# Gates' stage of a hybrid decoder block: the order of its products and weight sums, mixed results loaded as whole tiles, low parts on VectorE

## The chip, the cores and the metric

The kernel runs on one core of one Trainium2 chip. The time is that of one execution on the device, in microseconds (us), the median of several runs. The profile comes from one profiled execution of the kernel before the change, and every time below is from that execution unless it is called a median.

The names of the profile: PE is TensorE's matmul, PEld its weight load, DVE is VectorE, ACT is ScalarE, POOL is GpSimd, SP is SyncE, which issues nearly all DMAs. L255 is line 255 of the kernel.

## The reference

One decoder block on x of 2048 tokens by 1024 channels, all in float32. Cut to what matters:

```python
h = rmsnorm(x, attn_norm)
z = h @ w_in                         # pool | q | k | v | gate_pool | gate_attn
g_pool, g_attn = split(sigmoid(z[gates] + b_gate))
a = pool_mixer(u_pool, w_pool, pool_scale)
b = swa_sink_attention(rope(rmsnorm(q)), rope(rmsnorm(k)), v, sinks)   # window 128
x = x + (g_pool * a + g_attn * b) @ w_out
h = rmsnorm(x, ffn_norm)
up = causal_depthwise_conv(h @ w_up, conv_w, conv_b)
x = x + (silu(up[gate half]) * up[value half]) @ w_down
```

There are 16 query heads and 2 key and value heads of 64 channels, d_ff is 2816, and the pooling windows are 2, 4, 8 and 16.

## The kernel before

**Number format.** A float32 operand is split in a high part (a cast to float32r on ScalarE) and a low part (the operand less its high part, a subtraction on VectorE). A product is made of three matmuls: high by high, high by low, low by high. `split` (L229 to L234) makes both parts of a weight tile in two halves: L232 is the cast, L233 the subtraction. `split_added` (L236 to L240) makes the low part in another way, for the tiles of `pu` (eight), `q` (the first four), `ga` and `pg` (two each): ScalarE writes the high part (L238) and the negative of the high part (L239 copies with scale -1), and GpSimd issues a DMA (L240) that reads the weights again from memory and adds them. Only chunk 0 makes these tiles; chunk 1 loads the made ones back.

**Tiling and stages.** The tokens are cut in two chunks of 1024. Each chunk goes through: keys, values and queries, sliding-window attention with projections between its steps (`project` at L255, scores at L868, exponentials at L887, the probabilities' transposes at L901 and their copies at L903 and L906, GpSimd's select of the window's edge at L909, the values at L929); the Gates' stage; the output projection (`out_proj`, also L255); the up-projection; and the down-projection. Up and gates use a seven-product scheme for a 2 by 2 block product: each pair of output slabs needs the products "one" to "seven" (`class Up`), each of 12 matmuls of 512 columns, issued at L1164 in `product`.

**The Gates' stage.** It works through six units, u0 to u5, in the order of `UNITS`. A unit makes the two gates (attention and pool) of one slab of 128 channels. Its products add on PSUM banks: "one", "three", "five" and "seven" on one bank (`self.x`), each but the last two copied off by ScalarE (L1182, `kept`) before the next one writes; "four" and "six" on another (`self.z`), "four" copied off; "two" on a third. `early` is "six" issued ahead of its sum. VectorE adds the partial sums (L1194, L1208, L1220), and `sigmoid` multiplies by the norm's factor (L1370), takes tanh on ScalarE (L1371) and multiplies into the attention or pool result (L1372). `combine` (L1381) adds both and stores the slab to `xd` in memory. `fetch` loads the pool result `dd` and the attention result `tad`.

**Operands of that stage.** The left operands are sums of weight blocks, made by `Blocks` in four steps (L356 is the cast, L357 the subtraction for its low part, L372 and L373 the same for `A22`, L376 to L385 the sums). `weights(f, n)` runs n more steps for unit f. The right operands are blocks of the input, loaded by `load_input` (1 MB each), scaled by `scale_input` (L1406), combined (`right_t2`, `right_t3`, `right_t4`) and split by `parted` (L1039 the cast, L1040 the low part).

**The output projection.** It makes two halves of 512 tokens (n = 0, 1) by eight slabs (m). Each needs the four mixed results of that half in parts. Those of the first half are made at the end of the Gates' stage, those of the second at m = 1 to 4 of the first half: `mixed(j, n)` loads 512 KB of `xd` into an M tile and splits it.

**What sets the order.** Every engine runs its instructions in program order. A scheduler at build time interleaves the streams from the order of the code and the tile pools: "U" with 19 tiles of 1 MB, "M" with 5, "F" with 4, "R" with 3, "Q" with 6, and two PSUM banks each for f, a and t. A pool hands its slots out in the order of allocation, and a new tile waits for the last use of the slot's old one, be that a DMA.

Of the kernel before, what the change touches and what calls it, by code (L numbers as in the profile page):

```python
# [26 lines left out]
P = 128  # L27
D = 1024
S = 2048
T = 1024  # L30
# [175 lines left out]
def block_kernel(ctx: ExitStack, tc: tile.TileContext, x, xT, pos, vec, qkn, w_poolT, w_pool, w_q, w_kv,  # L206
# [21 lines left out]
    def split(hi, lo, src):  # L228
        n = src.shape[1] // 2  # L229
        for i in range(2):  # L230
            t = slice(i * n, (i + 1) * n)
            high = A.copy(hi[:, t], src[:, t])  # L232
            low = V.tensor_sub(lo[:, t], src[:, t], hi[:, t].bitcast(F32))  # L233
        return high.ins, low.ins  # L234

    def split_added(hi, lo, src, again):  # L236

        A.copy(hi, src)  # L238
        A.activation(lo, src, AF.Copy, scale=-1.0)  # L239
        G.dma_start(lo, again.bitcast(F32R), accum_op=ALU.add)  # L240

    def halves(h, t, src, gain):

        A.activation(h[:, 0, t], src, AF.Identity, scale=gain)
# [46 lines left out]

    def split_weights(key, raws):
        if key[0] in ("up", "gates"):
            return Blocks(raws)
        if key[0] == "none":
            return None
        out = []
        if raws is None:
            for src in made[key]:
                out.append(up_.tile(list(src.shape), F32R, "U"))  # L300
                load(out[-1].bitcast(F32), src)
            return out if len(out) > 1 else out[0]
        for raw in raws:
            shape = [P, 2] + list(raw.shape)[1:]
            p, tag = (mp, "M") if out and key[1] not in FOLDS[:FOLD_LEAD] else (up_, "U")
            out.append(p.tile(shape, F32R, tag))
# [29 lines left out]
    class Blocks:  # L336
# [23 lines left out]
        def step(self, n=1):  # L360
            for _ in range(n):
                if self.at < 4:
                    (self.first, self.second, self.third, self.fourth)[self.at]()
                    self.at += 1

        def first(self):
# [65 lines left out]
    class Input:  # L432
# [8 lines left out]
        def pair(self, j, n):  # L441
            return self.t[j, n]

        def fresh(self, k, n):
            if k % 2 == 0:
                self.t[k // 2, n] = up_.tile([P, 2, 2, 512], F32R, "U")
            return self.at(k, n)

    def make_h(c, n, hs, ks=range(KT)):

        a, b = ((0, 256), (256, 512), (512, T))[n] if c == 0 else (0, T)
        for k in ks:
            gain = vc[:, V_AN + k:V_AN + k + 1]
            if c == 0:
                h = hs.at(k, 0) if n == 1 else hs.fresh(k, n // 2)
                halves(h, slice(a % 512, a % 512 + b - a), xs0[k // 2][:, k % 2, a:b], gain)
            else:
                src = mp.tile([P, T], F32, "M")
                load(src, xT[k * P:(k + 1) * P, c * T:(c + 1) * T])
                for i in range(2):  # L460
                    halves(hs.fresh(k, i), slice(0, 512), src[:, 512 * i:512 * i + 512], gain)

    both = up_.tile([P, 2, 4, 2 * P], F32, "U")

# [586 lines left out]
    def out_proj(c, ms):  # L1051

        xg = [up_.tile([P, 2, T], F32, "U") for _ in range(4)]
        norms = []
        heads = [Kept(f) for f in PRE]
        for n in range(2):
            acc = fp.tile([P, 512], F32, "F")
            c_ = slice(n * 512, (n + 1) * 512)
            for m in range(KT):
                xr = fp.tile([P, 512], F32, "F")  # L1060
                load(xr, xT[m * P:(m + 1) * P, c * T + n * 512:c * T + (n + 1) * 512])
                w = stream.get("out", m)
                for f, at in PRE.items() if c == n == 0 else ():
# [276 lines left out]
    class Gates(Up):  # L1340
# [45 lines left out]
        def gate(self):  # L1386
            self.attn()
            self.combine()

        def parts(self, t):  # L1390

            k = self.f % 2
# [16 lines left out]
    def gates(c, units, b, xg, last_probabilities, last_values):  # L1409
# [36 lines left out]
        u1.five()  # L1446
        u0.gate()
        weights(2, 1)
        n = len(units)
        for f in range(2, n):  # L1450
            u, old = units[f], units[f - 1]
            if f > 2:
                u.one()
                u.two()
            old.fetch()
            weights(f + 1, 1)
            old.seven()
            old.value()
            weights(f + 1, 1)
            if f < n - 1:  # L1460
                u.three()
            else:
                u.four()
            weights(f + 1, 1)
            old.six()
            old.gate()
            weights(f + 1, 1)
            if f < n - 1:
                u.four()
            else:  # L1470
                u.three()
            u.five()
        ms = {j: [mixed(j, 0)] for j in (3, 2, 1)}
        x0 = up_.tile([P, 2, 2, 512], F32R, "U")
        old.parts(x0)
        stream.part(stream.used + 2)
        u.fetch()
        u.value(N1)
        u.seven()
        u.value(N0)  # L1480
        u.six()
        u.attn()
# [5 lines left out]
        return ms  # L1488

    ORDER = ("P1", "P2", "P6", "P5", "P7", "P3", "P4")  # L1490

# [248 lines left out]
    for c in range(NCH):  # L1740
        ms = mixer(c, hs, kvw)
        dn = Down(c)
        up(c, *out_proj(c, ms), dn)
        extra = []
        if c + 1 < NCH:
            hs = Input()
# [73 lines left out]
```

## Time and profile before

| | |
|---|---|
| median of three runs | 2435.97 us (2435.09 to 2445.2) |
| the profiled execution | 2440.7 us, span 2439.0 us, mean granted TensorE clock 0.994 |
| DMA traffic | 393.43 MB, mean 161 GB/s |
| matmuls | 11108 |

The stages by the trace, in us from the span's start: attention and what lies before it to 376 in chunk 0, the Gates' stage 376 to 505, the output projection 505 to 605, up to 1030, down to 1245; in chunk 1 attention to 1570, the Gates' stage 1570 to 1703, the output projection to 1800, up to 2225, down to the end. Matmuls overlap, so PE's busy time is a union and its mean duration of one is not the spacing. The granted clock stands in its own column (1.00 is full speed). The profile's waits name the releaser that came last.

### The profile page before, as it was taken

How to read it: one execution, taken by the hardware profiler on the slowest of the kernel's cores; microseconds unless marked ns; L12 is line 12 of the kernel's file. 1: busy time of each engine (PE TensorE's matmuls, PEld its weight loads, DVE VectorE, ACT ScalarE, POOL GpSimd, SP SyncE). 2: the span in 40 equal slices, each digit the busy share in tenths (PEclk: the TensorE clock that was granted, in tenths of full speed). 3: DMA queues.
4: the chain of work that ended last, by engine and by line, in shares of the span. 5: the costliest groups of instructions: out<-in, count | busy, mean ns of one | idle time of the engine just before them, and what ended most of it. 6: DMA issues, size and time to landing. Idle time of an engine off the chain costs nothing.

```text
span 2439.0 us, 30309 instructions
## 1 busy us (share of the span) xinstructions
PE 2383.8 (98%) x11108; PEld 1973.2 (81%) x11108; DVE 1888.0 (77%) x2902; ACT 1205.1 (49%) x2179; POOL 192.3 (8%) x134
## 2 busy tenths in 40 slices
PE   8999998989999999999999999989999999999999
PEld 7887886868888888888888888867788888888887
DVE  8677878877887777799956867887678777779994
ACT  6555556445555555543522544554545554554432
POOL 0124221000000000000002232200000000000000
PEclk9999999999999999999999999999999999999999
DMA  9689985588332233545244575545752222228421
GB/s 357 197 259 245 248 214 172 165 277 284 120 104 78 81 110 117 179 165 195 87 152 141 176 220 167 170 128 177 242 174 98 79 93 88 78 69 284 138 70 52
DMA packets 164341, 393.43 MB, mean 161 GB/s; under 512 B 14304, under 2 KB 50656, under 8 KB 156256
## 3 DMA queue, kind: packets, MB, share of 16 engines
q1 hardware_dynamic: 157104, 374.53, 45.9%
q0 software_dynamic: 6656, 16.78, 4.1%
q8 instruction: 87, 1.43, 0.2%
q14 instruction: 62, 0.51, 0.1%
q10 hardware_dynamic: 432, 0.19, 0.0%
HBM read 266.27 MB, written 125.17 MB: 160 GB/s over the span
## 4 chain that ended last, share of the span: by engine, by line
PE 51%; DMA 3%; DVE 2%; ACT 1%; issue 1%; POOL 0%; DVEq 0%; SPq 0%; ACTq 0%
PE f L255 11%; PE f L1164 10%; PE t L1164 5%; PE f L1614 4%; PE a L1614 4%; PE s L1614 4%; PE t L1614 4%; PE a L1164 3%; PE a L929 1%; PE a L255 1%; PE s L868 1%; PE t L901 0%; DMA M<-xd 0%; DMA F<-dd 0%; DMA U<-xT 0%
## 5 line engine op out<-in xcount | busy, mean ns | idle before, releaser
L255 PE MATMUL f<-U,U 128*128 128x512 f32 (+1 forms) x2784 | 654.7, 391 | 15.9 <-ACT U L232 7.6
L255 PEld LDWEIGHTS f<-U,U 128*128 128x128 f32 x2784 | 512.7, 189 | 125.5 <-ACT U L232 9.7
L1164 PE MATMUL f<-U,U 128*128 128x512 f32 x1872 | 447.6, 390 | 1.3 <-ACT Q L1182 1.3
L1164 PEld LDWEIGHTS f<-U,U 128*128 128x128 f32 x1872 | 350.8, 188 | 76.2 <-ACT Q L1182 3.0
L1230 DVE SCALAR_TENSOR_TENSOR M<-F,vc,M 128x1024 f32<-128x1024 f32 x176 | 225.1, 1281 | 140.9 <-ACT M L1227 140.5
L1164 PE MATMUL t<-U,U 128*128 128x512 f32 x1392 | 329.5, 391 | 2.1 <-ACT Q L1182 2.1
L1164 PEld LDWEIGHTS t<-U,U 128*128 128x128 f32 x1392 | 262.1, 189 | 58.1 <-ACT Q L1182 3.4
L356 ACT CAST U<-R 128x1024 fp32r<-128x1024 f32 x156 | 162.7, 1052 | 84.9 <-DVE R L377 46.5
L1164 PE MATMUL a<-U,U 128*128 128x512 f32 x768 | 190.5, 396 | 6.3 <-ACT Q L1182 5.3
L357 DVE TENSOR_TENSOR U<-R,U 128x1024 fp32r<-128x1024 f32 x156 | 190.2, 1220 | 1.2 <-ACT U L356 1.0
L1164 PEld LDWEIGHTS a<-U,U 128*128 128x128 f32 x768 | 146.0, 191 | 38.2 <-ACT Q L1182 6.2
L1164 PE MATMUL f<-U,M 128*128 128x512 f32 x624 | 151.0, 390 | 3.1 <-DVE F L1208 3.1
L887 ACT ACTIVATE Q<-s,st,rq 128x128 f32<-128x128 f32 x256 | 114.0, 457 | 56.3 <-DVE st L884 56.3
L1164 PEld LDWEIGHTS f<-U,M 128*128 128x128 f32 x624 | 116.9, 188 | 28.6 <-DVE F L1208 4.4
L909 POOL TENSOR_SCALAR_AFFINE_SELECT M<-M 128x1024 fp32r<-128x1024 f32 x64 | 97.6, 1525 | 333.0 <-DVE st L889 226.2
L1216 ACT COPY F<-f 128x512 f32<-128x512 f32 x52 | 30.6, 588 | 185.4 <-PE f L1164 185.4
L1572 ACT CAST U<-U 128x1024 fp32r<-128x1024 f32 x76 | 79.0, 1051 | 85.1 <-PE s L1614 21.0
L1227 ACT ACTIVATE M<-F,vc 128x1024 f32<-128x1024 f32 x88 | 109.4, 1243 | 2.0 <-DVE F L1212 0.5
L1573 DVE TENSOR_TENSOR U<-U,U 128x1024 fp32r<-128x1024 f32 x76 | 91.9, 1217 | 3.7 <-ACT U L1572 3.5
L1182 ACT COPY Q<-f 128x512 f32<-128x512 f32 x104 | 61.1, 588 | 65.1 <-PE f L1164 64.9
L1572 ACT CAST F<-U 128x1024 fp32r<-128x1024 f32 x44 | 46.2, 1049 | 90.6 <-PE a L1614 59.9
L936 ACT COPY U<-a 128x512 f32<-128x512 f32 x64 | 37.6, 587 | 101.5 <-PE a L929 101.3
(286 smaller groups left out, 3755.6 us busy)
## 6 DMA issues: line engine op xcount, KB each, us to landing
R<-w_up SPq DMA_DIRECT2D x80, 512.0 KB, 3.8
actd<-M SPq DMA_DIRECT2D x44, 512.0 KB, 2.6
U<-w_down SPq DMA_DIRECT2D x88, 256.0 KB, 5.2
U<-actd SPq DMA_DIRECT2D x88, 256.0 KB, 5.4
qd<-U SPq DMA_DIRECT2D x64, 256.0 KB, 3.8
Q<-qd SPq DMA_DIRECT2D x64, 256.0 KB, 5.3
R<-w_out SPq DMA_DIRECT2D x32, 512.0 KB, 4.8
U<-kept SPq DMA_DIRECT2D x12, 1024.0 KB, 6.6
```

The costliest lines, as they stand in the source:

```text
L255: nc.tensor.matmul(out, a, b, start=(i == 0), stop=(i == n - 1))
L356: A.copy(t[:, 0], raw)
L357: V.tensor_sub(t[:, 1], raw, t[:, 0].bitcast(F32))
L887: A.activation(pr[:, h, :], sc[:, h, 0:P], AF.Exp, bias=nm[:, h:h + 1], scale=it["rq"][:, h:h + 1], accum_out=rs[:, h:h + 1])
L909: G.affine_select(own.rearrange("p a h q -> p (a h) q"), pa.bitcast(F32).rearrange("p a h q -> p (a h) q"), pattern=[[0, 8], [1, P]], base ...
L1164: nc.tensor.matmul(bank, a[:, x, k, :], b[k // 2][:, y, k % 2, :], start=(first and i == 0), stop=(i == 11), skip_group_check=True)
L1182: Up.last = A.copy(t, bank).ins
L1227: A.activation(y, u[:, 2:], AF.Identity, bias=cw[:, 3, m:m + 1], scale=cw[:, 2, m:m + 1])
L1230: V.scalar_tensor_tensor(y, u[:, j:j + T], cw[:, j, m:m + 1], y, op0=ALU.mult, op1=ALU.add)
L1572: A.copy(hi, src)
L1573: V.tensor_sub(lo, src, hi.bitcast(F32))
L1614: nc.tensor.matmul(into[m], u[:, 0, c_], v[:, 1], start=(first and j == 0), stop=(k == n - 1 and j == 2), skip_group_check=True)
```

## The change

1. `split_added` is gone; its sixteen tiles go through `split`, so their low parts are VectorE's, two subtractions a tile.
2. `Blocks` of units 0 and 1 make S1 and S4 (`fourth`) ahead of S3 and S2 (`third`).
3. `gates` issues products, sums and weight steps in another order. In the steady loop it was one, two, seven of the unit before, three, six and the gate of the unit before, four, five. Now it is one, two, the attention gate of the unit before, its seven and value, three, four, its combine, five, early, and the sum of six. The second pair of input tiles is loaded ahead of u2's weights.
4. Mixed results 3, 2 and 1 are loaded whole, 1 MB in a U tile, during the last unit; the fourth at m = 3 of the output projection's first half. Both halves' parts are cut from the resident tiles, those of the second half at m = 4 to 7.
5. `Input.fresh` takes the tiles of both halves at once.

```diff
-            if key[0] in ("ga", "pg", "pu") or key[0] == "q" and key[1] < 4:
-                split_added(hi, lo, raw, slabs[key[0]][key[1]])
-            else:
-                split_weights.last = split(hi, lo, raw)
+            split_weights.last = split(hi, lo, raw)
...
-        def __init__(self, raws):
+        def __init__(self, raws, early=False):
             self.raws, self.w, self.at = raws, {}, 0
+            self.steps = [self.first, self.second] + [self.third, self.fourth][::-1 if early else 1]
...
-    def mixed(j, n):
-        t = mp.tile([P, 2, 512], F32, "M")
-        load(t, pair_of(xd, j)[:, :, n * 512:(n + 1) * 512])
-        return parted(t)
+    def mixed(j):
+        t = up_.tile([P, 2, T], F32, "U")
+        load(t, pair_of(xd, j))
+        return t
...
-                if n == 0 and m in (1, 2, 3, 4):
-                    ms[4 - m].append(mixed(4 - m, 1))
+                if n == 0 and m == 3:
+                    mixes[0] = mixed(0)
+                if n == 0 and m > 3:
+                    ms[7 - m].append(parted(mixes.pop(7 - m)[:, :, N1]))
...
         u0, u1, u2 = units[:3]
+        xg += [load_input(c, j) for j in (2, 3)]
         weights(2, 1)
         u2.one("t")
         last_probabilities()
-        weights(1, 1)
+        weights(1, 2)
         u2.two()
         last_values()
-        xg += [load_input(c, j) for j in (2, 3)]
         u0.four()
         u0.early()
-        weights(1, 2)
...
         u0.three()
         u0.six()
+        weights(1, 1)
         u0.five()
         right_t4(xg, b, t2s)
         u0.fetch()
-        weights(2, 1)
         u1.three()
+        u1.six()
+        u0.attn()
         u0.seven()
         u0.value()
         weights(2, 1)
-        u1.six()
         u1.five()
-        u0.gate()
-        weights(2, 1)
+        u0.combine()
+        weights(2, 2)
...
             old.fetch()
+            old.attn()
             weights(f + 1, 1)
+            if f == n - 1:
+                mixes = {j: mixed(j) for j in (3, 2, 1)}
             old.seven()
             old.value()
             weights(f + 1, 1)
-            if f < n - 1:
-                u.three()
-            else:
-                u.four()
+            u.three()
+            u.four()
+            old.combine()
+            if f == n - 1:
+                ms = {j: [parted(mixes[j][:, :, N0])] for j in (3, 2, 1)}
+                x0 = up_.tile([P, 2, 2, 512], F32R, "U")
+                old.parts(x0)
+                stream.part(stream.used + 2)
             weights(f + 1, 1)
-            old.six()
-            old.gate()
+            u.five()
+            u.early()
+            u.six()
             weights(f + 1, 1)
-            if f < n - 1:
-                u.four()
-            else:
-                u.three()
-            u.five()
```

How the build places the instructions, at three places. First ScalarE at the start of the Gates' stage of chunk 0, before (L1406 is the scaling of an input tile, L887 the exponentials, L1182 the copy of a product, L936 the copy of attention's values, L356 a weight's cast, L903 a copy of probabilities):

```order
L1406 ACTIVATE U_3916<-U_3916,vc_127 128x1024 x2
L936 COPY U_3946<-a_3941 128x4x128
L356 CAST U_3990<-R_3476 128x1024
L903 CAST M_3969<-t_3964 128x512
L1406 ACTIVATE U_3995<-U_3995,vc_127 128x1024
L887 ACTIVATE Q_3931,st_3927<-s_1581,st_3927,rq_207 128x128 x4
L890 ACTIVATE st_3927<-st_3927 128x4
L1182 COPY Q_3962<-f_3949 128x512
```

And now (the same lines are L1397, L880, L1177, L929, L1032 for L1039):

```order
L1397 ACTIVATE U_3934<-U_3934,vc_127 128x1024 x2
L880 ACTIVATE Q_3949,st_3945<-s_1583,st_3945,rq_207 128x128 x4
L883 ACTIVATE st_3945<-st_3945 128x4
L1177 COPY Q_3980<-f_3967 128x512
L929 COPY U_3964<-a_4036 128x4x128
L1397 ACTIVATE U_4011<-U_4011,vc_127 128x1024 x2
L1032 CAST U_4091<-U_3934 128x1024
```

The scaling of the second input tile (U_3995 before, U_4011 now) stood ahead of the group of four exponentials; now it stands behind them and behind the copy of a product (L1177).

Second, TensorE at the end of the Gates' stage of chunk 0, the last unit's products and the first of the output projection, before (f_4681 is the last unit's bank for three, five and seven; t_4730 the one for four and six; L255 the projection):

```order
L1164 MATMUL f_4681<-U_4187,U_4625 128x512 x6
L1164 MATMUL f_4681<-U_4192,U_4625 128x512 x6
L1164 MATMUL t_4730<-U_888,U_4648 128x512 x4
L1164 MATMUL f_4681<-U_4223,U_4625 128x512 x6
L1164 MATMUL f_4681<-U_4227,U_4625 128x512 x6
L1164 MATMUL t_4730<-U_888,U_4648 128x512 x2
L1164 MATMUL t_4730<-U_893,U_4648 128x512 x6
L1164 MATMUL f_4681<-U_4260,M_4606 128x512 x6
L1164 MATMUL f_4681<-U_4264,M_4606 128x512 x6
L255 MATMUL f_4876<-U_4793,U_4809 128x512 x6
```

And now (f_4710 and t_4782 are the same banks; L249 is the projection):

```order
L1159 MATMUL f_4710<-U_4200,U_4674 128x512 x6
L1159 MATMUL f_4710<-U_4205,U_4674 128x512 x6
L1159 MATMUL t_4782<-U_4091,U_4706 128x512 x6
L1159 MATMUL t_4782<-U_4095,U_4706 128x512 x6
L1159 MATMUL f_4710<-U_4236,U_4674 128x512 x6
L1159 MATMUL f_4710<-U_4240,U_4674 128x512 x6
L1159 MATMUL t_4782<-U_366,U_4706 128x512 x6
L1159 MATMUL t_4782<-U_372,U_4706 128x512 x6
L1159 MATMUL f_4710<-U_4276,M_4638 128x512 x6
L1159 MATMUL f_4710<-U_4280,M_4638 128x512 x6
L249 MATMUL f_4892<-U_4799,U_4811 128x512 x6
```

The twelve matmuls of "six" (right operand U_888 and U_893 before, U_366 and U_372 now) were partly ahead of "five" (U_4223, U_4227) and partly behind it; now "four" (U_4091, U_4095) stands between "three" and "five", and all of "six" between "five" and "seven" (U_4276, U_4280).

Third, ScalarE in the output projection of chunk 0, from the second slab on, before (L1085 scales the result, L642 and L645 are the squares for the norm, L232 casts weights, L356 makes sums of the up-projection's weights, L1039 cuts the parts of a mixed result in an M tile):

```order
L642 ACTIVATE F_4868<-M_4901 128x512
L232 CAST U_4906<-R_4871 128x512 x2
L356 CAST U_4915<-U_4873 128x1024
L1039 CAST U_4925<-M_4923 128x1024
L232 CAST U_4960<-R_4913 128x512 x2
L356 CAST U_4969<-U_4873 128x1024
L1085 ACTIVATE U_4864<-M_4953,vc_127 128x512
L645 ACTIVATE M_4956<-M_4953 128x512
L356 CAST U_4974<-U_4873 128x1024
L645 ACTIVATE M_5010<-M_5007 128x512
L1039 CAST U_4979<-M_4977 128x1024
```

And now (the same lines are L1080, L635 and L638, L232, L348; L1032 for L1039 comes later):

```order
L635 ACTIVATE F_4884<-M_4917 128x512
L232 CAST U_4922<-R_4887 128x512 x2
L348 CAST U_4931<-U_4889 128x1024
L232 CAST U_4971<-R_4929 128x512 x2
L348 CAST U_4980<-U_4889 128x1024
L1080 ACTIVATE U_4880<-M_4964,vc_127 128x512
L638 ACTIVATE M_4967<-M_4964 128x512
L348 CAST U_4985<-U_4889 128x1024
L1080 ACTIVATE U_4881<-M_5013,vc_127 128x512
L638 ACTIVATE M_5016<-M_5013 128x512
L232 CAST U_5020<-R_4978 128x512 x2
```

The casts from M tiles (U_4925 and U_4979) are gone from between the weights' casts.

More of the change, by code (lines that the diff above doesn't have):

```diff
@@ L234, in split @@
         return high.ins, low.ins
[L236 to L240, printed above, removed]
     def halves(h, t, src, gain):
@@ L293, in split_weights @@
         if key[0] in ("up", "gates"):
-            return Blocks(raws)
+            return Blocks(raws, key[0] == "gates" and key[1] < 2)
         if key[0] == "none":
@@ L362, in step @@
                 if self.at < 4:
-                    (self.first, self.second, self.third, self.fourth)[self.at]()
+                    self.steps[self.at]()
                     self.at += 1
@@ L442, in pair, with fresh @@
             return self.t[j, n]
-        def fresh(self, k, n):
+        def fresh(self, k):
             if k % 2 == 0:
-                self.t[k // 2, n] = up_.tile([P, 2, 2, 512], F32R, "U")
-            return self.at(k, n)
+                for n in range(2):
+                    self.t[k // 2, n] = up_.tile([P, 2, 2, 512], F32R, "U")
     def make_h(c, n, hs, ks=range(KT)):
@@ L453, in make_h @@
             gain = vc[:, V_AN + k:V_AN + k + 1]
+            if n == 0:
+                hs.fresh(k)
             if c == 0:
-                h = hs.at(k, 0) if n == 1 else hs.fresh(k, n // 2)
-                halves(h, slice(a % 512, a % 512 + b - a), xs0[k // 2][:, k % 2, a:b], gain)
+                halves(hs.at(k, n // 2), slice(a % 512, a % 512 + b - a), xs0[k // 2][:, k % 2, a:b], gain)
             else:
@@ L460, in make_h @@
                 for i in range(2):
-                    halves(hs.fresh(k, i), slice(0, 512), src[:, 512 * i:512 * i + 512], gain)
+                    halves(hs.at(k, i), slice(0, 512), src[:, 512 * i:512 * i + 512], gain)
     both = up_.tile([P, 2, 4, 2 * P], F32, "U")
@@ L1041, in parted, with out_proj @@
         return t
-    def mixed(j, n):
-        t = mp.tile([P, 2, 512], F32, "M")
-        load(t, pair_of(xd, j)[:, :, n * 512:(n + 1) * 512])
-        return parted(t)
+    def mixed(j):
+        t = up_.tile([P, 2, T], F32, "U")
+        load(t, pair_of(xd, j))
+        return t
     x2d = dp.tile([8, P, T], F32, "x2d")
-    def out_proj(c, ms):
+    def out_proj(c, ms, mixes):
         xg = [up_.tile([P, 2, T], F32, "U") for _ in range(4)]
@@ L1384, in combine @@
             load(xd[self.f][:, cs], self.ta[:, cs])
-        def gate(self):
-            self.attn()
-            self.combine()
         def parts(self, t):
@@ L1459, in gates @@
             weights(f + 1, 1)
-            if f < n - 1:
-                u.three()
-            else:
-                u.four()
+            u.three()
[6 more added lines that the diff above has]
+                stream.part(stream.used + 2)
             weights(f + 1, 1)
-            old.six()
-            old.gate()
+            u.five()
+            u.early()
+            u.six()
             weights(f + 1, 1)
-            if f < n - 1:
-                u.four()
-            else:
-                u.three()
-            u.five()
[L1473 to L1476, printed above, removed]
         u.fetch()
+        u.attn()
         u.value(N1)
@@ L1480, in gates @@
         u.value(N0)
-        u.six()
-        u.attn()
         for c_ in (N0, N1):
@@ L1487, in gates @@
         ms[0] = [x0]
-        return ms
+        return ms, mixes
     ORDER = ("P1", "P2", "P6", "P5", "P7", "P3", "P4")
@@ L1742, in block_kernel @@
         dn = Down(c)
-        up(c, *out_proj(c, ms), dn)
+        up(c, *out_proj(c, *ms), dn)
         extra = []
```

## The prediction

> **What bounds the kernel now.** First the page: which engine is full, and what the chain that ended last is made of.
>
> ```profile
> span 2439.0 us, 30309 instructions
> ...
> PE 2383.8 (98%) x11108; PEld 1973.2 (81%) x11108; DVE 1888.0 (77%) x2902; ACT 1205.1 (49%) x2179; POOL 192.3 (8%) x134
> ...
> PE 51%; DMA 3%; DVE 2%; ACT 1%; issue 1%; POOL 0%; DVEq 0%; SPq 0%; ACTq 0%
> ```
>
> TensorE is busy for 98%. The change takes no product away, so it can only win time in which TensorE stands still or runs at a lower clock, and only in its stages. So the second view is busy time by stage, the stages cut where the products change. The columns are the window, its length, then busy time (and count) of PE, PEld, DVE, ACT and POOL, the granted clock, the DMA share and GB/s.
>
> ```profile
> core 0: us, PE busy (x) PEld busy (x) DVE busy (x) ACT busy (x) POOL busy (x), PEclk, DMA share, GB/s
> 110.00:220.00 110.00, 108.78 (x560) 90.93 (x560) 75.06 (x153) 61.99 (x159) 38.07 (x22) 1.00 0.86 243
> 220.00:300.00 80.00, 76.25 (x382) 63.76 (x382) 62.91 (x124) 42.66 (x123) 28.14 (x19) 0.98 0.89 245
> 300.00:376.00 76.00, 75.22 (x386) 62.99 (x385) 58.43 (x124) 41.94 (x120) 18.12 (x16) 1.00 0.85 231
> 376.00:426.00 50.00, 41.52 (x170) 31.63 (x169) 38.83 (x52) 29.25 (x50) 6.63 (x4) 0.93 0.52 159
> 426.00:505.00 79.00, 79.00 (x350) 65.27 (x349) 63.67 (x69) 36.49 (x44) 0.00 (x0) 1.00 0.51 168
> 505.00:560.00 55.00, 45.85 (x180) 34.65 (x179) 42.45 (x58) 30.18 (x45) 0.00 (x0) 0.94 0.85 296
> 1330.00:1570.00 240.00, 238.34 (x1243) 201.56 (x1242) 185.16 (x363) 107.91 (x350) 62.89 (x37) 1.00 0.58 171
> 1570.00:1625.00 55.00, 47.41 (x200) 36.88 (x200) 44.12 (x63) 34.17 (x62) 8.28 (x6) 0.94 0.57 165
> 1703.00:1735.00 32.00, 28.44 (x120) 21.65 (x119) 23.05 (x32) 16.21 (x26) 0.00 (x0) 1.00 0.69 226
> ```
>
> I read the time lost in a window as its length less PE's busy time, plus its length times what is missing in the clock. The steady part of the Gates' stage, 426 to 505, loses nothing: 350 matmuls in 79.00 us, 226 ns each. Its start in chunk 0 (376 to 426) loses 8.5 idle and 50 x 0.07 = 3.5 in clock, 12.0. The start in chunk 1 (1570 to 1625) loses 7.6 + 3.3 = 10.9. The end of the stage with the first rows of the output projection loses 9.2 + 3.3 = 12.5 in chunk 0 (505 to 560) and 3.6 in chunk 1 (1703 to 1735). Check of the third: 180 matmuls at 226 ns are 40.6 us, and the window is 55, so 14.4 are lost; the method is up to 2 us low.
>
> Which waits these are, the view of waits on TensorE says, first for 220 to 605, then for 1330 to 1800 (total, times, longest, in us).
>
> ```profile
> PE f L255 <- ACT U L232: 5.8, 3, 3.4
> PE f L255 <- DMA U<-w_ga: 3.7, 1, 3.7
> PE s L868 <- ACT Q L887: 2.6, 2, 2.2
> PE a L929 <- POOL M L909: 2.6, 3, 1.6
> PE a L1164 <- ACT Q L1182: 2.5, 1, 2.5
> PE f L255 <- DVE U L233: 2.0, 2, 1.5
> PE f L1164 <- DVE F L1208: 1.1, 1, 1.1
> ```
>
> ```profile
> PE a L1164 <- ACT Q L1182: 2.8, 1, 2.8
> PE f L255 <- ACT U L232: 1.8, 2, 1.0
> PE f L1164 <- DVE F L1208: 1.6, 1, 1.6
> ```
>
> ScalarE, 49% busy, is named most often, so it must itself stand in a queue behind something. Its own waits in 376 to 605 say behind what:
>
> ```profile
> ACT U L1039 <- DMA M<-xd: 11.2, 4, 5.0
> ACT U L1039 <- DMA tad<-U: 4.5, 1, 4.5
> ACT U L1406 <- DMA U<-xT: 4.5, 1, 4.5
> ```
>
> Three kinds of cast wait for transfers, in program order ahead of copies and exponentials that TensorE needs. Last, what follows a gap:
>
> ```profile
> 233.50:238.00 4.50, 4.32 (x12) 3.42 (x13) 2.63 (x4) 0.00 (x0) 0.69 (x1) 0.62 1.05 316
> 387.00:391.50 4.50, 4.50 (x20) 3.73 (x19) 4.47 (x6) 3.42 (x6) 0.00 (x0) 0.62 0.59 204
> 416.00:419.00 3.00, 0.49 (x4) 0.07 (x2) 0.51 (x1) 1.58 (x3) 0.00 (x0) 0.94 0.79 309
> 419.00:421.00 2.00, 2.00 (x5) 1.61 (x6) 2.00 (x3) 0.95 (x2) 0.00 (x0) 0.50 0.03 12
> ```
>
> After 2.5 idle us (416 to 419) the clock is at half from 419 to 421. A wait here costs itself and 1 to 2 us of low clock, which go with it.
>
> The Trainium skill, page "TensorE: Matmul & The Clock Gate", section on the HAM clock gate, has the clock halve after an idle window of about 3.4 us. This trace halves it after 2.5, so the measurement decides; by the page's rule the 2 to 2.8 us waits would not be what lowers the clock, 4.3 us of clock counted below would stay, and the sum below would be -19.5 instead of -23.8.
>
> **The change part by part.** Low parts on VectorE (chunk 0's attention). Sixteen tiles lose a ScalarE pass and an accumulating DMA issued by GpSimd, and gain two VectorE subtractions each.
>
> ```profile
> DMA to landing us min/median/max: 6.5/9.0/10.6
> ...
> L233 DVE TENSOR_TENSOR U<-R,U x86: 675/683/695, 7.3 to 1788.1; 128x512 fp32r<-128x512 f32 x86
> ...
> L373 DVE TENSOR_TENSOR M<-R,M x52: 653/684/1577, 364.8 to 2190.5; 128x512 fp32r<-128x512 f32 x52
> ```
>
> The first line is those accumulating transfers, 9.0 us each. One was late: the 3.7 us wait on w_ga, and with the clock after it (4.5 x 0.38 = 1.7) it costs 5.4. It goes: **-5.4**. Added are 32 x 0.683 = 21.9 us of VectorE. From 110 to 376 it is busy for 75.1 + 62.9 + 58.4 = 196.4 of 266 us (74%); it becomes 82%. What does that cost TensorE? No row shows 82%. The nearest is chunk 1's attention, 185.16 of 240 (77%), where TensorE idles for 1.7 us; in chunk 0, without w_ga, it idles 5.8 - 3.7 = 2.1 at 74%. The least is 0; the most is that in each of 16 tiles one subtraction delays a softmax step that TensorE waits for, 16 x 0.683 = 11. A gain is excluded for these additions, since VectorE only gets more. I take **+2**, near the 77% row.
>
> The last line above is the same form as the subtraction: 684 ns at the median, 1577 at most. That instruction ran beside a GpSimd select. The Trainium skill, page "GPSIMD Engine Reference", section 8, says that GpSimd shares its SBUF interfaces with VectorE and contends with VectorE instructions that have two SBUF inputs, which the new subtractions are. It speaks against the change, and the 1577 agrees with it; its price is in the first rival.
>
> Start of the Gates' stage, chunk 0. (a) The exponentials (L887) stood behind the input scaling (L1406), which waited 4.5 us for xT; scores then waited 2.2. The changed order has the exponentials ahead of that second input and the loads earlier: -2.2, and the clock of 387 to 391.5, 4.5 x 0.38 = 1.7. (b) Product "early" of unit u1 waited 2.5 us for ScalarE's copy, which stood behind a cast (L1039) that waited 4.5 us for a tile slot held by the transfer of tad. Slots are handed out in order of allocation; with the input tiles allocated earlier, the slot held by that transfer falls to a later cast (a T4 part), behind the copy, and T4's user is a product further on. -2.5, and 2.0 x 0.5 = 1.0 of clock. What stays: the select on GpSimd (2.6), and the copy between u0.four and u0.early, which are still neighbours on one bank. New: the weight cast for u2.one now stands behind exponentials; between 0 and 1.9 us (the longest waits of this kind above are 1.6 and 2.2), I take 1. Sum **-6.4**; between -3 and -9.
>
> Chunk 1 has the same order. Its copy wait is 2.8, half of its 3.3 of clock follows that one; less 0.4 for the new wait: **-4**; between -1 and -7.
>
> Last unit and output projection. The last "seven" waited for the sum (L1208) that freed its bank, 1.1 and 1.6 us; in the changed order "early", 12 x 226 ns = 2.7 us, stands between "five" and "seven", which covers both. The weights' casts (L232) stood behind casts of M tiles whose xd transfers waited 11.2 us in four; now those parts are cut from tiles that are resident by then. In chunk 0 the waits are 5.8 + 2.0 + 1.1 = 8.9 of the 9.2 idle; with the clock 12.5. DMA share stays near 0.85, so I leave 1.5 for a late w_out: **-11** (-5 to -12.5). Chunk 1: 1.8 + 1.6, less 0.4: **-3** (-1 to -3.6). The whole tiles have a price: their casts now wait for 1 MB, and the nearest 1 MB load takes 7.6 us:
>
> ```profile
> U<-xT SPq DMA_DIRECT2D x8, 1024.0 KB, 7.6
> ```
>
> The first is issued about two groups of 12 matmuls (5.4 us) ahead of its cast and the other two right behind it. The casts stand on ScalarE ahead of the tanh and the copy of "three", for which "five" waits, and that copy has a group of 2.7 us as cover. A first cast 7.6 - 5.4 = 2.2 late and two of the same size behind it would use that up: between 0 and 4 us a chunk, I take 1 for each, **+2**.
>
> Steady loop. Before, two groups of 12 stood between "three" and "five"; now one, "four". "five" needs the copy of three's sum, and ScalarE has that copy behind the tanh of the gate that ended before.
>
> ```profile
> 453.92 2.88 PE L1164 MATMUL f<-U,U 128*128 128x512 f32 x12
> 456.63 5.60 PE L1164 MATMUL t<-U,U 128*128 128x512 f32 x24
> 462.07 1.30 PE L1164 MATMUL f<-U,U 128*128 128x512 f32 x5
> ...
> 457.20 1.15 ACT L1371 ACTIVATE F<-F,vc 128x1024 f32<-128x1024 f32 x1 [1.41 <-DVE F L1370]
> 458.26 0.57 ACT L1182 COPY Q<-f 128x512 f32<-128x512 f32 x1
> ```
>
> "three" runs from 453.92, the copy ends at 458.83, and "five" starts at 462.07. With 12 matmuls fewer it would start at 462.07 - 2.71 = 459.36: 0.5 us to spare. Over eight such units some will miss it: from 0 to 8 x 1.5 = 12, I take **+2**. Taking both halves of an input tile at once changes no engine's order before 109 us: 0; the slots that it holds longer lie in the folding at the start.
>
> Sum: -5.4 + 2 - 6.4 - 4 - 11 - 3 + 2 + 2 = -23.8. The profiled execution took 2440.7 us (1.7 around the span), so 2416.9 for it; the median of the runs, 2435.97, lies 4.7 below it, and a new median should too: 2435.97 - 23.8 = 2412.2.
>
> **The rivals.** First, VectorE in chunk 0's attention: POOL is busy for 84.3 of 266 us there, so a third of the 32 subtractions take 1.58 instead of 0.68 (9 us more), softmax steps run late, and the +2 becomes +11: 2421. Against it: 77% cost chunk 1 only 1.7. Second, the waits come back in another place: the 1 MB loads land late at the last unit in both chunks, and the -14 of the output projection becomes -4: 2422. For it: DMA share 0.85. Third, slower: the copy of "three" is late in each of the eight units. It decides from 0.5 us late on; the gain is used up at (23.8 + 2) / 8 = 3.2 us a unit. At 3 us and 1.5 of low clock each it gives 36 instead of 2: +10.2, 2446. Against it: VectorE is at 63.67 of 79 us in the steady part, which leaves no such queue for tanh. Fourth, the order doesn't do what it says: the cast that waits for tad's slot still stands ahead of the copy in both chunks; then -2.5 - 1.0 and -4 go: 2412 + 7.5 = 2420.
>
> **How the numbers follow.** The forecast has 0.58 (2403 to 2419), the first rival 0.15, the second 0.12, the fourth 0.10, the slower one 0.05. What a measurement of this kernel can tell from no change is about 0.5%, 12.2 us: faster is under 2423.8. The first, second and fourth rival stay under it alone; two of them together, or one with a gain at its low end, do not, and I give that 0.15. So faster 0.80, same 0.15, slower 0.05. For the range the low end is the sum without its three costs (-6) and with the far ends of the gains in both starts (-2.6 and -3) and in the projection (-1.5 and -0.6): 2412 - 14 = 2398; the high end is the first two rivals together, 2412 + 19 = 2431.
>
> **What would show it.** Right: no wait on w_ga; PE busy without a gap between scores and u1's "early" but for the select; no ScalarE wait on xd in the output projection; its first 55 us 11 shorter. Wrong: PE waits for low parts or for exponentials between 110 and 376; "five" waiting for the copy in the steady loop; ScalarE waiting for whole xd tiles at the last unit; a wait on tad ahead of a copy.

## The result, and the profile after

The changed kernel takes 2421.18 us (median of four runs, 2419.71 to 2424.93) against 2438.77 for the kernel before (four runs): a ratio of 0.9927, 95% interval 0.9901 to 0.9954. That is 17.6 us, 0.7%; the forecast was 23.8, and 2412.2 as a time. The profiled span went from 2439.0 to 2419.2, by 19.8. One run of the kernel before, in a later batch, took 3166.89 us at a granted clock of 0.70 and is left out of every ratio. The page of the changed kernel:

```profile
span 2419.2 us, 30260 instructions
...
PE 2376.2 (98%) x11108; PEld 1971.5 (81%) x11108; DVE 1906.2 (79%) x2934; ACT 1187.9 (49%) x2179; POOL 178.4 (7%) x118
```

VectorE has 32 instructions and 18 us more, ScalarE 17 us less. Busy time by stage, in windows near those of the prediction; they do not hold the same matmuls, as the counts show, so rows of the two kernels can't be subtracted (the first column is the window, then its length, PE, PEld, DVE, ACT, POOL, clock, DMA share, GB/s):

```profile
110.00:220.00 110.00, 108.51 (x557) 90.47 (x555) 82.63 (x167) 56.53 (x160) 31.38 (x15) 1.00 0.70 211
220.00:300.00 80.00, 79.93 (x414) 67.53 (x414) 70.77 (x144) 39.12 (x127) 24.54 (x13) 1.00 0.77 237
300.00:372.00 72.00, 72.00 (x371) 60.95 (x370) 61.19 (x127) 36.49 (x113) 16.59 (x12) 1.00 0.65 178
372.00:419.00 47.00, 39.80 (x164) 30.71 (x163) 37.48 (x50) 30.12 (x51) 5.22 (x4) 0.93 0.58 182
419.00:498.00 79.00, 79.00 (x350) 65.43 (x349) 69.02 (x78) 38.55 (x49) 0.00 (x0) 1.00 0.61 206
498.00:553.00 55.00, 50.70 (x218) 39.93 (x217) 43.32 (x59) 32.47 (x49) 0.00 (x0) 1.00 0.86 310
1550.00:1610.00 60.00, 52.02 (x232) 41.59 (x231) 50.43 (x70) 36.69 (x66) 8.33 (x6) 0.94 0.60 180
1684.00:1716.00 32.00, 31.88 (x141) 25.95 (x140) 21.57 (x31) 15.90 (x27) 0.00 (x0) 1.00 0.68 218
```

The attention (first three rows) and the output projection of chunk 1 (1684 to 1716) lost most of their idle time, that of chunk 0 (498 to 553) about half. The two starts of the Gates' stage (372 to 419, 1550 to 1610) look as before: 7.2 and 8.0 us idle, at a clock of 0.93 and 0.94.

To compare kernels I use one number for each stage, **lost time**: over all matmuls in it, the spacing to the next one less the undisturbed spacing (0.227 us for 512 columns, 0.119 for 256, 0.064 for 128). Idle time and low clock are in it together, and in the attention also matmuls that stand wider apart with TensorE busy: of the 14.0 left there, only 1.6 is idle (busy 260.4 of 262 us). Stages are cut at the same count of matmuls in each kernel, so the rows can be subtracted. In us:

| kernel | attention, chunk 0 | Gates' start, 0 | projection, 0 | Gates' start, 1 | projection, 1 | whole span |
|---|---|---|---|---|---|---|
| before | 20.0 | 15.0 | 15.4 | 13.6 | 6.1 | 115.2 |
| changed | 14.0 | 12.7 | 8.4 | 12.8 | 1.3 | 95.1 |
| low parts only | 14.2 | 14.0 | 12.9 | 14.7 | 5.2 | 107.2 |
| Gates' order only | 19.6 | 11.1 | 12.7 | 13.0 | 5.0 | 107.6 |
| changed, old mixes | 14.1 | 12.7 | 13.7 | 11.9 | 4.9 | 103.4 |
| changed, low parts twice | 20.0 | 11.4 | 11.3 | 9.9 | 1.3 | 100.5 |
| changed, earlier load | 14.1 | 9.0 | 9.4 | 6.5 | 1.5 | 87.8 |
| changed, weight first | 14.1 | 11.8 | 9.5 | 10.4 | 1.3 | 94.1 |
| changed, load and weight | 14.1 | 6.6 | 11.4 | 6.2 | 1.2 | 87.6 |
| changed, both loads and weight | 14.1 | 7.9 | 10.3 | 9.8 | 1.6 | 90.6 |
| earlier load, casts first | 14.1 | 8.8 | 8.6 | 8.4 | 1.5 | 86.5 |

A stage that an edit doesn't touch still differs by 1 to 3 us between builds (the projection of chunk 0 above all), so a single cell is worth no more than that. The runs come from four batches, in which the kernel before came out between 2438.49 and 2441.22, so a difference between medians of two batches is good to 2 or 3 us only; the last column is the cross-check.

What TensorE waits for in the two starts now, chunk 0 first (360 to 420), then chunk 1 (1545 to 1610):

```profile
PE s L861 <- ACT Q L880: 2.5, 1, 2.5
PE t L1159 <- ACT U L348: 1.8, 1, 1.8
PE f L1159 <- ACT Q L1177: 1.7, 1, 1.7
PE t L1159 <- ACT Q L1177: 0.7, 1, 0.7
```

```profile
PE s L861 <- ACT Q L880: 3.1, 1, 3.1
PE t L1159 <- ACT U L348: 1.8, 1, 1.8
PE f L1159 <- ACT Q L1177: 1.5, 1, 1.5
```

Scores still wait for exponentials, in chunk 1 for 3.1 us where the longest such wait before was 0.8. ScalarE's own waits say why; the first two are chunk 0's, the third chunk 1's:

```profile
ACT U L1397 <- DMA U<-xT: 3.7, 1, 3.7
ACT U L1032 <- DMA tad<-U: 3.3, 1, 3.3
```

```profile
ACT U L1397 <- DMA U<-xT: 4.6, 1, 4.6
```

And the timeline of ScalarE in the changed kernel:

```profile
376.53 2.19 ACT L1397 ACTIVATE U<-U,vc 128x1024 f32<-128x1024 f32 x2 [3.73 <-DMA U<-xT]
378.63 0.44 ACT L880 ACTIVATE Q<-s,st,rq 128x128 f32<-128x128 f32 x1
```

The exponentials stand behind the scaling (L1397) of the first input tile, and that waits for its load. SyncE's queue, before and now, shows the load's place in it:

```profile
364.76 0.39 SPq L226 DMA_DIRECT2D U<-xT  x1
368.77 0.58 SPq L226 DMA_DIRECT2D tad<-U  x1
372.35 0.34 SPq L226 DMA_DIRECT2D R<-w_gp  x1
```

```profile
361.81 0.58 SPq L226 DMA_DIRECT2D tad<-U  x1
362.50 0.55 SPq L226 DMA_DIRECT2D Q<-qd  x1
366.80 0.34 SPq L226 DMA_DIRECT2D R<-w_gp  x1
367.23 0.90 SPq L226 DMA_DIRECT2D U<-xT  x2
```

Before, the first load of xT left ahead of tad's store and of a weight's load; now it leaves behind both. The weight's load leaves 4.3 us after the load ahead of it, right when VectorE has read the old R tile (L349 ends at 366.77): it waits for its slot, and everything behind it waits too.

### The profile page after: what moved, and what is told of

Its sections match the earlier page's. It is cut to its first block, busy times and chain, and to the rows that moved or that the text cites. A ratio compares the mean times of both kernels' runs of the same rounds, so it can differ in the third digit from the quotient of the medians.

```text
span 2419.2 us, 30260 instructions
## 1 busy us (share of the span) xinstructions
PE 2376.2 (98%) x11108; PEld 1971.5 (81%) x11108; DVE 1906.2 (79%) x2934; ACT 1187.9 (49%) x2179; POOL 178.4 (7%) x118
## 4 chain that ended last, share of the span: by engine, by line
PE 88%; DVE 4%; DMA 3%; ACT 3%; issue 1%; POOL 0%; SPq 0%; DVEq 0%; ACTq 0%
PE f L1159 22%; PE f L249 22%; PE t L1159 13%; PE a L1159 6%; PE f L1603 4%; PE a L1603 4%; PE s L1603 4%; PE t L1603 4%; PE a L922 2%; PE s L861 2%; PE a L249 1%; PE t L894 1%; DMA U<-xT 1%; DMA tad<-U 1%; ACT Q L880 0%
## 5 line engine op out<-in xcount | busy, mean ns | idle before, releaser
L249 PE MATMUL f<-U,U 128*128 128x512 f32 (+1 forms) x2784 | 649.2, 389 | 7.5 <-ACT U L232 3.4
L249 PEld LDWEIGHTS f<-U,U 128*128 128x128 f32 x2784 | 510.2, 188 | 113.4 <-DVE U L233 4.9
L348 ACT CAST U<-R 128x1024 fp32r<-128x1024 f32 x156 | 163.1, 1053 | 72.3 <-DVE R L377 37.4
L349 DVE TENSOR_TENSOR U<-R,U 128x1024 fp32r<-128x1024 f32 x156 | 190.7, 1226 | 2.7 <-ACT U L348 2.7
L880 ACT ACTIVATE Q<-s,st,rq 128x128 f32<-128x128 f32 x256 | 113.8, 456 | 53.1 <-DVE st L877 52.7
L929 ACT COPY U<-a 128x512 f32<-128x512 f32 x64 | 37.6, 588 | 117.5 <-PE a L922 117.3
L1177 ACT COPY Q<-f 128x512 f32<-128x512 f32 x104 | 60.8, 585 | 60.7 <-PE f L1159 60.6
```

The source lines that it names most:

```text
L249: nc.tensor.matmul(out, a, b, start=(i == 0), stop=(i == n - 1))
L348: A.copy(t[:, 0], raw)
L349: V.tensor_sub(t[:, 1], raw, t[:, 0].bitcast(F32))
L880: A.activation(pr[:, h, :], sc[:, h, 0:P], AF.Exp, bias=nm[:, h:h + 1], scale=it["rq"][:, h:h + 1], accum_out=rs[:, h:h + 1])
L1177: Up.last = A.copy(t, bank).ins
```

## The experiments

My theory after the result: the low parts, the whole tiles and the Gates' order each give part of the gain, and the Gates' starts gave little because new waits on ScalarE's queue took the place of those removed. The main rival is the prediction's first: VectorE takes back part of the gain.

**The low parts alone**, in the kernel before.

```diff
-            if key[0] in ("ga", "pg", "pu") or key[0] == "q" and key[1] < 4:
-                split_added(hi, lo, raw, slabs[key[0]][key[1]])
-            else:
-                split_weights.last = split(hi, lo, raw)
+            split_weights.last = split(hi, lo, raw)
```

> The kernel before with only the low parts moved to VectorE. My theory: the 3.7 us wait on w_ga and its low clock go and VectorE's 22 us more cost TensorE nothing, so the attention of chunk 0 loses about 6 us less, Gates' stage and output projection lose what they lost before: 5 to 7 us faster in all, 0.2 to 0.3%. Rival, VectorE late in softmax: TensorE waits for low parts or exponentials between 110 and 376, the same time as before or up to 5 us slower.

Measured 2432.92 us, ratio 0.9971 (0.9958 to 0.9984), 7 us. The attention of chunk 0 loses 14.2 instead of 20.0: the wait on w_ga and its low clock, and nothing back from VectorE. The theory holds.

**Twice the subtractions**, in the changed kernel.

```diff
-            low = V.tensor_sub(lo[:, t], src[:, t], hi[:, t].bitcast(F32))
+            for _ in range(times):
+                low = V.tensor_sub(lo[:, t], src[:, t], hi[:, t].bitcast(F32))
```

`times` is 2 for the sixteen tiles and 1 for all others.

> The changed kernel in which each of the 32 new subtractions is issued twice with the same operands: VectorE in chunk 0's attention goes from 82% to 90%. If VectorE has room there, TensorE loses at most 2 us more than in the changed kernel. Rival of the prediction, VectorE becomes the bound: softmax steps run late, TensorE waits for low parts and exponentials, 5 to 15 us slower than the changed kernel.

Measured 2426.69 us, ratio 0.9943 (0.9928 to 0.9958): 5.5 us more than the changed kernel's median, and 20.0 lost in chunk 0's attention instead of 14.0. The stage in this run, and its waits on VectorE:

```profile
110.00:220.00 110.00, 107.83 (x545) 88.63 (x544) 90.53 (x179) 55.94 (x159) 32.77 (x15) 1.00 0.70 210
220.00:300.00 80.00, 78.24 (x404) 65.66 (x403) 75.92 (x149) 38.51 (x124) 23.84 (x13) 1.00 0.71 216
300.00:376.00 76.00, 74.06 (x381) 62.26 (x381) 66.00 (x134) 37.66 (x118) 17.68 (x13) 1.00 0.63 184
```

```profile
PE t L896 <- DVE Q L888: 3.0, 5, 1.2
PE s L865 <- DVE st L886: 1.8, 2, 1.3
```

VectorE is busy for 90.5 + 75.9 + 66.0 = 232 of 266 us, 87% (not the 90% reckoned ahead, since the stage grew). The first dose, to 82%, cost nothing; the second costs 6 us, spread over softmax steps. So the rival names a true mechanism, and here its point lies between 82% and 87%; the change stops short of it.

**The mixed results as before**, in the changed kernel: halves of 512 KB in M tiles, at the end of the Gates' stage and at m = 1 to 4.

```diff
-                if n == 0 and m == 3:
-                    mixes[0] = mixed(0)
-                if n == 0 and m > 3:
-                    ms[7 - m].append(parted(mixes.pop(7 - m)[:, :, N1]))
+                if n == 0 and m in (1, 2, 3, 4):
+                    ms[4 - m].append(mixed(4 - m, 1))
```

> The changed kernel with mixed results loaded as before, in halves of 512 KB in M tiles (it computes the same). My theory: ScalarE again waits for xd in the output projection and weights' casts stand behind that; chunk 0's projection loses 4 to 8 us more than in the changed kernel and chunk 1's 1 to 3 more: 5 to 10 us slower than the changed kernel. Rival, the gain there came from putting early between five and seven: the same time as the changed kernel within 2 us.

Measured 2429.88 us, ratio 0.9948 (0.9928 to 0.9968): 8.7 us over the changed kernel's median. The projection loses 13.7 and 4.9 instead of 8.4 and 1.3, and the wait on xd is back on ScalarE:

```profile
ACT U L1032 <- DMA M<-xd: 6.0, 3, 4.2
```

Of the 7.0 and 4.8 us won there, 5.3 and 3.6 are the whole tiles', as the theory has it. The edit changes size, pool and time of these loads together, so which of the three matters is not shown.

**The Gates' order alone**, in the kernel before: low parts and mixed results are its own, the edit is the change's in `Blocks`, `Input` and `gates`. Against the changed kernel it puts these back:

```diff
-            split_weights.last = split(hi, lo, raw)
+            if key[0] in ("ga", "pg", "pu") or key[0] == "q" and key[1] < 4:
+                split_added(hi, lo, raw, slabs[key[0]][key[1]])
+            else:
+                split_weights.last = split(hi, lo, raw)
...
-                ms = {j: [parted(mixes[j][:, :, N0])] for j in (3, 2, 1)}
+                ms = {j: [mixed(j, 0)] for j in (3, 2, 1)}
```

> The kernel before with only the Gates' stage in its new order (low parts and mixed results as before). If the three parts add up: the low parts gave 7 us and the whole tiles 8.7, so this one should be 2 to 4 us faster than the kernel before. Rival, the new order needs VectorE's low parts to pay: the same time as before within 1 us, or slower.

Measured 2433.28 us, ratio 0.9980 (0.9967 to 0.9992): 5 us, more than the 2 to 4 expected, and not nothing, as the rival had it. In lost time the three parts are 8.0, 8.3 and 7.6 us, together 23.9 against 20.1 for the change: they nearly add up. Most of the 3.8 too much lies in the projection; that the parts took some of the same waits there is not shown, since it is no more than builds differ by.

**The first input tile loaded a step earlier**, in the changed kernel.

```diff
+                if n == 4:
+                    xg.append(load_input(c, 0))
                 if 3 <= n < 7:
...
                 if n == 5:
                     run_later(9)
                     units[1].w.step(1)
-                    xg.append(load_input(c, 0))
```

> The changed kernel with the first input tile of the Gates' stage loaded one attention step earlier (n = 4 instead of 5). My theory: the new wait of scores for exponentials (2.7 us in chunk 0, 3.3 in chunk 1) comes from the scaling ahead of them on ScalarE, which waits for that load; with the load landed, both waits and 1 to 1.5 us of low clock behind each go: 6 to 9 us faster than the changed kernel. Rival, the exponentials are late because of their own chain on VectorE: the waits stay, within 2 us of the changed kernel. A second rival, the second input tile's scaling takes its place: half of the gain.

Measured 2413.05 us, ratio to before 0.9882 (0.9866 to 0.9897), 8.1 us less than the changed kernel's median. The two starts lose 9.0 and 6.5 instead of 12.7 and 12.8:

```profile
372.00:416.00 44.00, 39.46 (x168) 30.19 (x167) 38.11 (x52) 28.64 (x49) 5.76 (x4) 0.96 0.60 178
1550.00:1605.00 55.00, 51.07 (x234) 40.51 (x233) 51.12 (x71) 37.47 (x67) 7.85 (x6) 1.00 0.60 168
```

In chunk 1 the wait on exponentials is gone, and the clock stays at 1.00. In chunk 0 the second rival is half right: ScalarE now waits as long for the second tile ahead of the exponentials, but only one pass of 1.15 us stands between, and scores wait 0.6. The first line is ScalarE's wait, the second TensorE's:

```profile
ACT U L1397 <- DMA U<-xT: 3.7, 1, 3.7
```

```profile
PE s L861 <- ACT Q L880: 0.6, 1, 0.6
```

This is the best of the versions that differ from the change by one edit; it beats both kernels.

**The weight step of u2 ahead of the last scores**, in the changed kernel.

```diff
                 if n == 7:
                     scale_input(xg[1], 1)
+                    units[2].w = stream.get("gates", 2)
+                    units[2].w.step(1)
...
-        weights(2, 1)
         u2.one("t")
```

> The changed kernel with the first weight step of unit u2 issued ahead of the last scores instead of behind the input loads. My theory: TensorE's wait for that cast (1.96 us in chunk 0, 1.93 in chunk 1) and the low clock after it go: 3 to 5 us faster than the changed kernel. Rival, the cast ahead of the exponentials makes them 1.05 us later and the wait comes back there: within 1 us of the changed kernel.

Measured 2419.79 us, ratio 0.9904 (0.9885 to 0.9924), 1.4 us under the changed kernel's median, which these runs can't tell from nothing. The wait on the cast is gone. In chunk 0 the exponentials are waited for as before, and a new wait came:

```profile
PE s L861 <- ACT Q L880: 2.4, 1, 2.4
PE a L922 <- POOL M L902: 2.1, 1, 2.1
```

The rival has the size right, not the place: the wait on exponentials did not grow (2.4 us against 2.5, and 1.6 against 3.1 in chunk 1). The select on GpSimd, which the values need, comes late; why is not shown.

**Both edits**, the earlier load and the weight step, and then the second input tile a step earlier too. The second run's edit on top of the first:

```diff
                 if n == 5:
                     run_later(9)
                     units[1].w.step(1)
+                    xg.append(load_input(c, 1))
                 if n == 6:
                     scale_input(xg[0], 0)
-                    xg.append(load_input(c, 1))
```

> The changed kernel with both edits of the two runs before: the first input tile loaded one attention step earlier and u2's first weight step ahead of the last scores. If the two waits are separate costs, the edits add up: 8 us from the load, 1.4 from the weight, 9 to 10 us faster than the changed kernel. Rival, the slot held by the transfer of tad: in this build it falls to a weight tile of u1's three, ahead of the copy that u0's five needs, so a wait of 1 to 2 us on one of them takes the gain of the weight step: 6 to 8 us faster than the changed kernel.

> As the run with the earlier load and the weight step, with the second input tile loaded a step earlier too (n = 5 instead of 6). If the second tile's scaling still holds back exponentials there, 1 to 3 us faster than that run; if its load had landed anyway, the same time within 1 us.

Measured 2414.21 us (0.9885, 0.9870 to 0.9900) and 2417.05 us (0.9897, 0.9881 to 0.9914). The first is not better than the earlier load alone: the starts lose 6.6 and 6.2, less than with the load alone (9.0 and 6.5), but chunk 0's projection 11.4 instead of 9.4. The rival had the size right; its mechanism is there, a weight's cast that waits 1.2 us for tad's transfer in chunk 0, but "five" waits only 0.7 us behind it where it waited 1.7, so that part of it falls. The second came out 2.8 us slower than the first, against both expectations, though the two intervals overlap; it loses 9.8 instead of 6.2 in chunk 1's start. Its trace shows why: a scaling stands ahead of the exponentials again, and waits 3.7 us for its load in chunk 0 and 3.5 in chunk 1, so scores wait 2.5 and 1.7. In the first run chunk 0's scaling (378.70) stands behind the exponentials (from 375.73). The second tile's load did not even leave earlier: it leaves right behind the load of w_gp in chunk 0, at 367.85 in the first run and at 367.02 in the second.

**The casts of the next weights ahead of a row's scaling** in the output projection, on top of the earlier load.

```diff
+                stream.part(stream.used + 2)
                 x2 = mp.tile([P, 512], F32, "M")
...
                 load(x2d[m][:, c_], x2)
-                stream.part(stream.used + 2)
```

> The kernel with the earlier input load, and in the output projection the cast of the next weights issued ahead of the scaling of a row's result instead of behind it. My theory: of the 10.7 us that chunk 0's projection still loses, most is the weights' cast standing on ScalarE behind a scaling that waits for VectorE, which waits for a late x row; with the cast ahead, 3 to 6 us faster than the run with the earlier load alone. Rival, the weights themselves land late, because the DMA queues are busy for 0.85 of that stage: within 2 us of it.

Measured 2411.82 us (0.9891, 0.9871 to 0.9911), the same as without it (2413.05), and chunk 0's projection loses 8.6 instead of 9.4. The rival has the size right. VectorE and ScalarE wait for transfers there, more for a row of x than for the weights that the rival named:

```profile
DVE M L1080 <- DMA F<-xT: 4.5, 2, 4.1
...
ACT U L232 <- DMA R<-w_out: 1.6, 2, 1.5
```

## Why the prediction was right or wrong

The direction, the size within the range and the first cause were right. The time by itself would not show it: 2421.18 is 9 us above the forecast and within 1.2 of the first, second and fourth rival (2421, 2422, 2420). The runs decide between them. Term by term, in lost time:

- **w_ga and VectorE: -5.4 and +2 forecast, -6.0 in all measured** (20.0 to 14.0). The wait went as worked out. The +2 was not there; the doubled dose shows that the bound of +11 wasn't idle, since 22 us more would have cost 6. One new subtraction did run beside a GpSimd select, 1575 ns against a median of 683; the rival had reckoned with a third of the 32:

```profile
L233 DVE TENSOR_TENSOR U<-R,U x118: 653/683/1575, 7.3 to 1768.4; 128x512 fp32r<-128x512 f32 x118
```

- **Start of the Gates' stage, chunk 0: -6.4 forecast, -2.3 measured; chunk 1: -4 forecast, -0.8 measured.** Here two steps failed. Step (a) said that the exponentials now stand ahead of the second input's scaling "and the loads earlier". The first half is true, the second was never looked up: the first tile's scaling still stands ahead of that group of exponentials (the rows quoted with the change show it), and its load had moved behind tad's store and a weight's load in SyncE's queue. The earlier load gives 3.7 us back in chunk 0 and 6.3 in chunk 1. Step (b) was right about the slot: the cast that waits for tad's transfer (3.3 us) is now T4's, and u1's "early" waits for nothing. But the copy of "three", for which "five" waits, stands behind that same cast, 1.7 and 1.5 us: a wait on tad ahead of a copy, the fourth rival's sign, on another copy than the one it named; I had looked for the slot's user, a product further on, and not for what is queued behind it. The new wait for u2's cast was taken as 1 in chunk 0 and 0.4 in chunk 1, and is 1.8 in both. The 2.7 us of low clock that was to go in chunk 0 did not: 47 x 0.07 = 3.3 is left of 3.5.
- **Last unit and projection: -11 and -3 forecast, -7.0 and -4.8 measured.** No wait for xd holds TensorE any more, and the sum ahead of "seven" holds it for 0.3 us at most. In chunk 0 the term was right for the rows that it was worked out from and missed what lies behind them. Here are the same matmuls in both kernels, the prediction's 55 us and the rest of the projection, before and then now:

```profile
505.20:560.10 54.90, 45.75 (x179) 34.58 (x178) 42.38 (x58) 30.18 (x45) 0.00 (x0) 0.94 0.86 297
560.10:605.10 45.00, 45.00 (x205) 37.33 (x205) 30.62 (x44) 23.52 (x39) 1.43 (x1) 1.00 0.85 285
497.20:540.20 43.00, 41.28 (x180) 33.12 (x179) 31.88 (x45) 22.63 (x35) 0.00 (x0) 1.00 0.84 303
540.20:590.10 49.90, 46.07 (x205) 36.99 (x204) 36.23 (x51) 27.84 (x45) 1.03 (x1) 1.00 0.83 280
```

The first part is 11.9 us shorter, as the prediction's sign had it; the second, which lost nothing, is 4.9 longer. There its weights' parts come late, and TensorE waits 3.8 us for them; ScalarE waits 2.7 us for w_out up to there, VectorE 3.6 for a row of x, at a DMA share of 0.83. With the old halves the second part takes 45.0 us again (551.2 to 596.2), so this loss comes with the whole tiles. Whether their loads hold up the others, or TensorE has only caught up with loads that were late before, is not shown.

- **Steady loop +2: 0. The whole tiles +2: 0 at the place forecast.** The casts of whole tiles wait 1.2 and 1.4 us for xd at the last unit and hold nothing up; what came back with them is the 4.9 us above: the second rival's kind of loss, in another place. The steady loop has 350 matmuls in 79.00 us, as before. TensorE and ScalarE at "three", "four" and "five" of one unit:

```profile
448.68 2.88 PE L1159 MATMUL f<-U,U 128*128 128x512 f32 x12
451.40 2.88 PE L1159 MATMUL t<-U,U 128*128 128x512 f32 x12
454.12 2.20 PE L1159 MATMUL f<-U,U 128*128 128x512 f32 x9
```

```profile
451.95 0.57 ACT L1177 COPY Q<-f 128x512 f32<-128x512 f32 x1
```

The copy ends at 452.52 and "five" starts at 454.12: 1.6 us to spare where 0.5 was worked out. The copy ends 3.8 us after "three" starts, where the row that I took had 4.9. That this is due to the attention gate, which now goes ahead of "seven", fits but was not tested. The slower rival was far off.

The sum came near partly by luck, since the errors cancel in part: 7.3 us too much in the starts and 2.2 in the projection, against 2.6 too little for the low parts and 4 for the two costs that did not come where they were looked for.

## What to carry to other kernels

When a stall is "engine A waits for B, which stands behind C", look at all that still stands ahead of B in the new order, and at where C's transfer stands in the queue that issues it: here a wait of the same size came back behind the next instruction of the same kind. Freed slots and moved loads change what waits, not only how long; follow the slot's new user and everything queued behind it on its engine. Before more work goes to an engine that is nearly full, double the added work once: it shows how near the limit is. And where a stall goes, look at the stretch behind it too: part of the gain can be given back there.

## What the runs showed of the hardware that was not expected

VectorE at 82% of a stage of short dependent steps held up nothing that these runs can tell, and at 87% it cost TensorE 6 us in 266. And the low clock does not go by the length of a gap alone, as the prediction took it (a wait costs itself and 1 to 2 us of clock). In the changed kernel half clock came behind the wait of 2.5 us (the first row) and behind the one of 1.8 (the second), but not behind one of 1.7, in the same stage, nor behind one of 1.9 (the third):

```profile
381.80:385.20 3.40, 3.40 (x12) 2.67 (x10) 3.35 (x6) 2.74 (x3) 0.00 (x0) 0.50 1.02 418
392.00:395.40 3.40, 3.40 (x10) 2.64 (x9) 2.54 (x4) 2.39 (x3) 0.60 (x1) 0.50 0.00 0
549.20:553.00 3.80, 3.42 (x14) 2.53 (x15) 3.80 (x6) 3.11 (x5) 0.00 (x0) 1.00 1.04 438
```
